# Output projection of an encoder block: eight half-size products become seven, with merged blocks summed in place and operands in reused rooms

## The chip, the cores and the metric

The kernel runs on one core of a Trainium2 chip. The core has a matrix engine (TensorE, PE in the profile, with its weight loads as PEld), an elementwise engine (VectorE, DVE), an engine for activations and copies (ScalarE, ACT), a programmable engine that is used for elementwise work here (GpSimd, POOL) and a queue that issues the DMAs (SyncE, SP). The on-chip memory is SBUF; products are accumulated in PSUM, which has eight banks of 128 x 512 float32 values. The metric is the time of one execution in microseconds on the device; the median of several runs is what counts.

## The reference

One encoder block on 1024 tokens of width 1024, with 16 meta tokens in front. Two attention branches give `y_a` and `y_b` (1024 x 512 each for the real tokens). What the change touches is the merge of the branches, the output projection, the residual, the norm and the beginning of the feed-forward:

```python
    merged = jax.nn.sigmoid(ga) * (y_a @ w_ba) + jax.nn.sigmoid(gb) * (y_b @ w_bb)
    return merged @ w_o
...
def swiglu(h, w_gate, w_up, w_down):
    return (jax.nn.silu(h @ w_gate) * (h @ w_up)) @ w_down
...
        h = h + mixer_block(rms_norm(h, norm_mix[layer]), w_in[layer],
...
        h = h + swiglu(rms_norm(h, norm_ffn[layer]), w_ff_gate[layer], w_ff_up[layer], w_ff_down[layer])
    return rms_norm(h, norm_final)[:, N_META:]
```

`w_o` is 1024 x 1024, the feed-forward is 2816 wide, all values are float32.

## The kernel before

Every product is made from float32 operands that are split into a high and a low half of type float32r: `split` writes the high half on ScalarE (L117) and the difference on VectorE or GpSimd (L118). A product of two operands is then three matmuls, high x high, high x low and low x high. The unit of work is a matmul of a 128 x 128 stationary block with a 128 x 512 moving block.

The program is traced in one function. Instructions of TensorE stay in the order of the program text from L1015 on (a manual order), and from L1370 on those of all engines do. Elsewhere a scheduler puts each engine's instructions in order, earlier text first among those that it takes to be ready. Each engine then works through its own list strictly in that order. Tiles come from pools: a tile with a tag takes one of the tag's rooms, and its first writer waits until the readers of the room's last tenant are done.

The stages around the change, in order:

1. *Branch b* (L1017): for each of eight blocks `o` of 128 output columns and two halves of the tokens, twelve matmuls (`branch_mm`, L780) into a PSUM bank; the result times the sigmoid of a gate goes to `tb_row(o, tk)` (L1021). The rows of `tb` lie in a tile of their own (`o` of 0 to 3) and in two rooms of `lowpool` (4 to 7).
2. *Branch a and merge* (L1037): the same for the other branch, in the order `order_a`: for blocks 0 to 3 and then 4 to 7, the first half of the tokens, then the second. VectorE multiplies with the gate (L1041), GpSimd adds the row of branch b (L1042), and the sum is split into `mT` (16 splits, the low half on VectorE). In the second half of this loop `prep_wo(0, c)` loads and splits the left half of `w_o`.
3. *Output projection* (L1241): `out_mm` multiplies one block of 128 tokens with one half (`q`) of the columns of `w_o`, over eight blocks `c` of the inner dimension, three matmuls each. Three rounds take four token blocks at a time, (q, group) = (0, 0), (0, 1), (1, 0); in the round (0, 1) `prep_wo(1, c)` prepares the other half of `w_o`. The last four token blocks follow one at a time (L1252). After a round `out_add` (L1075) adds the PSUM result to `h2`, which was loaded from `x`.
4. *Norm and turning*: `norm_f(t)` (L1199) squares and sums on ScalarE (L1202), takes the inverse root on GpSimd (L122, L123) and scales on VectorE (L1204) into a raw tile `xn`; `h2` goes out to DRAM. `turn_f(t)` (L1208) transposes eight 128 x 128 blocks on TensorE into two PSUM banks. For token blocks 0 to 3 it writes the operands `b11` and `b21` (L1222, L1223) and a copy `kept` (L1225). For blocks 4 to 7 it writes `b22` and four sums (L1233 to L1236). Blocks 0 to 4 are turned between the last output steps, blocks 5 to 7 between the first feed-forward products (`AFTER`, L1341), where `split_t` also splits the sums into the operands `t_ops`.
5. *Feed-forward, first half* (L1342): gate (`i` = 0) and up (`i` = 1) projections for eleven pairs `fp` of column blocks, each by seven half-size products in place of eight (`product_f`, twelve matmuls, L1293). The first, second and fifth product open a PSUM bank (`b1`, `b2`, `b3`); the others accumulate on in one of these. The products 1 and 2 of the first three pairs come first, so that the first-product banks of three pairs are open at a time. `result` empties banks: L1302 and L1307 add a kept copy, L1309 multiplies. `prepare` makes the weight operands up to eight ahead (`weights`, `load_unit`).
6. *Feed-forward, second half* (L1443): the down projection, also as seven products, and the final norm.

Rooms matter for the change. `op_tile` has eight rooms for split weights and `raw_tile` five for raw loads and for `xn`. `WB_BUFS` is the number of split branch weights held at a time (L773). `ps_bank` (L958) hands out any of eight PSUM banks. Separate pools hold `mT`, `gffn` and the first feed-forward weights (`mpool`), the operands `b11`, `b21`, `b22` (`bops`), eight tiles for `h2`, `kept` and the sums (`h2pool`), the operands of the sums (`topool`), the copies of products (`pcopy`, seven rooms) and the weight sums (`spool`).

## Time and profile before

| | us |
|---|---|
| median of three runs | 1451.38 |
| lowest and highest of the three | 1447.25, 1451.52 |
| profiled execution, whole | 1446.1 |
| profiled execution, first to last instruction (span) | 1444.3 |

The mean granted clock of TensorE in the profiled execution is 0.997. In a row of the page or of the windows, an engine's name is followed by its busy time and its number of instructions. In a group of instructions the row has line, engine, operation, written tile, read tiles, shapes and count, then the busy time and the mean of one in ns, then the engine's idle time just before and what ended it. In the order of instructions a row has its start, its time, the engine and line, and in brackets the idle time before it and what ended that. The chain of waits goes back from the last instruction to what released each one.

The stages in the trace: branch b from 622.0 us, branch a from 665.6, the first output matmul at 709.3 and the last at 800.6, the feed-forward from 801.6, the down projection from about 1227.

### The profile page before, as it was taken

The numbers are of one execution on the slowest core, as the hardware profiler recorded it, in microseconds if no ns is written. First come the engines' busy times: TensorE is split into PE (matmuls) and PEld (weight loads), VectorE is DVE, ScalarE is ACT, GpSimd is POOL, SyncE is SP. The second block draws the span as 40 slices with busy tenths as digits, with TensorE's granted clock in tenths as the row PEclk, the third lists the DMA queues.
The fourth block names the chain that finished last, engine by engine and source line by source line (L and its number), as shares of the span: only waits on it lengthen the run. The fifth ranks groups of instructions, "written<-read, shape, count | busy, mean of one in ns | idle before, by whom it ended". The sixth has DMA issues, their size and how long they took to land.

```text
span 1444.3 us, 21160 instructions
## 1 busy us (share of the span) xinstructions
PE 1422.8 (99%) x7279; PEld 1221.2 (85%) x7279; DVE 899.2 (62%) x1624; ACT 679.6 (47%) x1290; POOL 641.3 (44%) x605
## 2 busy tenths in 40 slices
PE   8999999999999999999999999999999999999997
PEld 6988989988898999888888878888888888888886
DVE  7478536637697989624614966554555553787567
ACT  6366535545665656544413643333333333444454
POOL 5599127743333333334522665544544452000444
PEclk9999999999999999999999999999999999999999
DMA  8467658986557473576612534333332332964443
GB/s 244 90 209 237 193 162 265 288 281 213 190 169 257 147 227 125 190 256 209 216 34 88 152 104 161 109 102 110 102 102 96 110 102 102 331 208 140 124 129 139
DMA packets 188891, 242.41 MB, mean 168 GB/s; under 512 B 18208, under 2 KB 115936, under 8 KB 188784
## 3 DMA queue, kind: packets, MB, share of 16 engines
q1 hardware_dynamic: 188784, 241.07, 52.6%
q8 instruction: 57, 0.93, 0.3%
q14 instruction: 50, 0.41, 0.1%
HBM read 157.45 MB, written 77.00 MB: 162 GB/s over the span
## 4 chain that ended last, share of the span: by engine, by line
PE 81%; POOL 6%; DVE 5%; issue 4%; DMA 2%; ACT 1%; POOLq 0%; SPq 0%; DVEq 0%; ACTq 0%
PE pg L1293 28%; PE pd L1387 9%; PE pg L737 7%; PE po L1070 6%; PE ppa L780 6%; PE aps L796 3%; PE pp_qb L214 3%; POOL oa L118 3%; PE apy L835 3%; PE pp_ka L214 2%; PE pp_va L214 2%; PE apt L822 2%; PE pp_qa L214 2%; PE bpt L356 1%; PE bpy L362 1%
## 5 line engine op out<-in xcount | busy, mean ns | idle before, releaser
L118 POOL TENSOR_TENSOR wop<-wf,wop 128x512 fp32r<-128x512 f32 x128 | 172.6, 1353 | 165.5 <-ACT wop L117 149.6
L1293 PE MATMUL pg<-t,wop 128*128 128x512 f32 x1056 | 242.6, 389 | 0.0
L1293 PEld LDWEIGHTS pg<-t,wop 128*128 128x128 f32 x1056 | 198.3, 188 | 41.1
L1387 PE MATMUL pd<-ob,oa 128*128 128x512 f32 x924 | 209.9, 389 | 0.4 <-POOL oa L118 0.4
L1387 PEld LDWEIGHTS pd<-ob,oa 128*128 128x128 f32 x924 | 173.4, 188 | 36.8 <-POOL oa L118 0.8
L1293 PE MATMUL pg<-b,wop 128*128 128x512 f32 x792 | 185.6, 392 | 2.3 <-DVE c L1302 2.3
L1293 PEld LDWEIGHTS pg<-b,wop 128*128 128x128 f32 x792 | 149.5, 189 | 34.1 <-issue 2.4
L737 PE MATMUL pg<-hT_hi,gop 128*128 128x512 f32 x384 | 142.7, 396 | 0.0
L118 POOL TENSOR_TENSOR oa<-ra,oa 128x512 fp32r<-128x512 f32 x33 | 44.0, 1335 | 170.1 <-ACT oa L117 168.6
L117 ACT ACTIVATE wop<-wf 128x512 fp32r<-128x512 f32 x128 | 80.2, 631 | 82.9 <-PE pg L1293 48.6
L118 POOL TENSOR_TENSOR gop<-gr,gop 128x512 fp32r<-128x512 f32 x48 | 63.3, 1319 | 116.4 <-ACT gop L117 102.6
L117 ACT ACTIVATE oa<-ra 128x512 fp32r<-128x512 f32 x77 | 48.7, 632 | 105.9 <-PE pd L1387 45.1
L804 ACT ACTIVATE as<-as,amn 128x1040 f32<-128x1040 f32 x64 | 74.5, 1164 | 46.9 <-DVE amn L799 42.8
L1128 DVE TENSOR_TENSOR s<-wf,wf 128x512 f32<-128x512 f32 x22 | 25.0, 1138 | 108.1 <-DMA wf<-in_w_ff_gate_dram 58.0
L796 PE MATMUL aps<-ak,aq 128*128 128x392 f32 (+1 forms) x384 | 90.0, 330 | 1.3 <-DVE amn L799 0.6
L1070 PE MATMUL po<-woh,mT 128*128 128x512 f32 x384 | 88.0, 390 | 0.0
L1070 PEld LDWEIGHTS po<-woh,mT 128*128 128x128 f32 x384 | 71.9, 188 | 14.8
L796 PEld LDWEIGHTS aps<-ak,aq 128*128 128x128 f32 x384 | 69.6, 189 | 15.0 <-DVE amn L799 2.2
L737 PEld LDWEIGHTS pg<-hT_hi,gop 128*128 128x128 f32 x384 | 72.7, 189 | 11.2 <-DVE gk L742 0.2
L343 POOL TENSOR_SCALAR bs<-bs,bdn 128x432 f32<-128x432 f32 (+1 forms) x64 | 41.4, 666 | 85.5 <-DVE bdn L341 73.4
L737 PE MATMUL pg<-hT_lo,gop 128*128 128x512 f32 x192 | 76.0, 396 | 0.0
L807 POOL TENSOR_SCALAR as<-as,adn,neglam 128x1040 f32<-128x1040 f32 x32 | 38.8, 1214 | 62.5 <-DVE adn L805 43.9
(287 smaller groups left out, 3099.0 us busy)
## 6 DMA issues: line engine op xcount, KB each, us to landing
ra<-aop SPq DMA_DIRECT2D x77, 256.0 KB, 2.6
wf<-in_w_ff_gate_dram SPq DMA_DIRECT2D x24, 512.0 KB, 4.0
wf<-in_w_ff_up_dram SPq DMA_DIRECT2D x24, 512.0 KB, 3.9
aop<-as SPq DMA_DIRECT2D x44, 256.0 KB, 2.1
w_c<-in_w_in_dram SPq DMA_DIRECT2D x17, 512.0 KB, 5.7
aop<-c SPq DMA_DIRECT2D x33, 256.0 KB, 2.0
ts_d<-to SPq DMA_DIRECT2D x16, 512.0 KB, 3.7
gw<-in_w_in_dram SPq DMA_DIRECT2D x32, 256.0 KB, 3.9
```

The costliest lines, as they stand in the source:

```text
L117: nc.scalar.activation(hi, src, AF.Copy)
L118: lo_eng.tensor_tensor(lo, src, f32(hi), ALU.subtract)
L214: nc.tensor.matmul(ps[:, :n], a[:, c, :], b[:, c, at:at + n], start=(c == 0 and i == 0), stop=(c == DC - 1 and i == 2))
L343: nc.gpsimd.tensor_scalar(st[:, r, :W], st[:, r, :W], dn[:, r:r + 1], 1.0, ALU.mult, ALU.mult)
L737: nc.tensor.matmul(ps, op[:, a, c], quad(b, *act)[:, c], start=(p in (2, 5, 1) and c == 0 and i == 0), stop=(p in (2, 3, 4) and c == 3 and ...
L780: nc.tensor.matmul(ps, w[:, a, j, :], src(j, b, tk), start=(j == 0 and n == 0), stop=(j == 3 and n == 2))
L796: nc.tensor.matmul(ps[:, :n], qs[m][:, t * P:(t + 1) * P], ks[m][:, vv, k0:k0 + n], start=(vv == 0), stop=(vv == 1))
L804: nc.scalar.activation(s[m][:, 0:L], s[m][:, 0:L], AF.Exp, bias=low, scale=-1.0, accum_out=dn[:, m:m + 1])
L835: nc.tensor.matmul(py[:, cols], v[:kp, a, k, :], at_[:kp, k, b, :], start=(k == 0 and j == 0), stop=(k == 8))
L1070: nc.tensor.matmul(ps, mT[:, c, a, t * P:(t + 1) * P], wos[q, c][:, b], start=(c == 0 and n == 0), stop=(c == DC - 1 and n == 2))
L1293: nc.tensor.matmul(ps, op[:, x, c, :], b[:, y, c, :], start=(p in (1, 2, 5) and c == 0 and n == 0), stop=(p in (4, 2, 3) and c == 3 and n ...
L1387: nc.tensor.matmul(ps[u], oa[:, a, u * P:(u + 1) * P], ob[:, b, :], start=(p in (1, 2, 5) and j == 0 and k == 0), stop=(p in (2, 3, 4) and ...
```

## The change

The output projection is cut into halves of the tokens, of the inner dimension and of the columns. Seven products of half-size operands, in the order `OUT` = 1, 5, 6, 3, 7, 2, 4, take the place of eight. Each product has four inner blocks, four token blocks and three matmuls. On the merged side, products 1, 3 and 2 use blocks of the merge as they are, and 5, 6, 7 and 4 use sums, which `m_sum` makes on VectorE in the place of the blocks. On the weight side, 5, 6, 3 and 7 use sums, made in `prep_wo`. Products 1, 6, 7 and 4 accumulate in one set of four banks (`xb`), 5 and 3 in another, 2 in a third; `out_add` reads a bank after each product. Products 2 and 4 go one token block at a time, and blocks 0 to 4 are turned among them, block 4 behind the last step.

The merge loop goes by quarters: second half of the tokens for blocks 0 to 3, first half for 0 to 3, first half for 4 to 7, second half for 4 to 7. GpSimd adds in the row of `tb`, and each quarter's split goes to the operand of one product (the second quarter by way of `m_sum(5, o)`). `load_ya` and `split_ya` take the second half of the tokens first.

The rooms: PSUM has two tags of four banks; the gate takes the one and the up projection the other, the turnings among the output steps use the first, and everything else alternates. `m_ops` and the operands of the feed-forward share rooms (`oa` to `oe`, the room of `tb`, and `gp`, which also holds `gffn`, the weight sums `s_f` and the first feed-forward weights). `h2` of blocks 4 to 7, the sums of the turned blocks and `s1` use the rooms of the split branch weights, four instead of five. The copies of products lie in two rooms of `lowpool`, four copies to a tile.

```diff
-WB_BUFS = 5
+WB_BUFS = 4
...
-    def ps_bank(name):
-        return bank(psum3, "bank", name, 8)
+    n_bank = [0]
+
+    def ps_bank(name, tag=None):
+        if tag is None:
+            tag = ("bankA", "bankB")[n_bank[0] % 2]
+            n_bank[0] += 1
+        return bank(psum3, tag, name, 4)
...
+    def prep_wo():
+        if n_wo[0] == len(order_o):
+            return
+        p, c = order_o[n_wo[0]]
+        n_wo[0] += 1
+        tt = nc.vector.tensor_tensor
+        raw = raw_tile(f"wo_{p}_{c}")
+        if p in (1, 6):
+            src = wo_block(raw, 0, c, 0)
+        elif p in (3, 2):
+            src = wo_block(raw, 0, 4 + c, 0)
+        elif p == 5:
+            a, b = wo_block(raw, 0, c, 1), wo_block(raw, 1, 4 + c, 1)
+            src = s_f[c]
+            tt(src, a, b, ALU.add)
+        elif p == 7:
+            src, b = wo_block(raw, 0, c, 0), wo_block(raw, 1, c, 1)
+            tt(src, src, b, ALU.subtract)
+        else:
+            src = wo_block(raw, 0, 4 + c, 1)
+        if p == 6:
+            tt(s_f[c], s_f[c], src, ALU.subtract)
+            src = s_f[c]
+        elif p == 3:
+            tt(src, src, s_f[c], ALU.subtract)
+        wos[p, c] = op_tile(f"woh_{p}_{c}")
+        split(wos[p, c][:, 0], wos[p, c][:, 1], src, nc.gpsimd)
...
+    def m_split(p, c, src):
+        split(m_ops[p][:, 0, c], m_ops[p][:, 1, c], src, nc.vector)
+
+    def m_sum(p, c):
+        tt = nc.vector.tensor_tensor
+        t, bx, b21 = tb_row(c, Y), tb_row(c, X), tb_row(4 + c, X)
+        if p == 5:
+            tt(t, t, bx, ALU.subtract)
+        elif p == 6:
+            tt(t, tb_row(4 + c, Y), t, ALU.subtract)
+        elif p == 7:
+            tt(bx, t, bx, ALU.subtract)
+            t = bx
+        else:
+            tt(b21, b21, t, ALU.subtract)
+            t = b21
+        m_split(p, c, t)
...
-    order_a = [(o, h) for b in range(0, DC, 4) for h in range(2) for o in range(b, b + 4)]
+    order_a = [(o, half) for b, halves in ((0, (1, 0)), (4, (0, 1))) for half in halves for o in range(b, b + 4)]
...
-        nc.gpsimd.tensor_tensor(gt, gt, tb_row(o, tk), ALU.add)
-        split(mT[:, o, 0, tk], mT[:, o, 1, tk], gt, nc.vector)
+        nc.gpsimd.tensor_tensor(tb_row(o, tk), tb_row(o, tk), gt, ALU.add)
+        if n // 4 == 1:
+            m_sum(5, o)
+        else:
+            m_split((1, None, 3, 2)[n // 4], o % 4, tb_row(o, tk))
         if n >= 8:
-            prep_wo(0, n - 8)
+            prep_wo()
...
+    xb = [ps_bank(f"po_x{u}", "bankB") for u in range(4)]
+    yb_ = [ps_bank(f"po_y{u}", "bankA") for u in range(4)]
+    for p in (1, 5, 6, 3, 7):
+        pss = yb_ if p in (5, 3) else xb
+        for c in range(4):
+            for u in range(4):
+                out_mm(pss[u], p, u, c)
+            prep_wo()
+            if p == 1:
+                m_sum(6, c)
+        for u in range(4):
+            if p == 1:
+                out_add(xb[u], 4 + u, 0)
...
+            else:
+                out_add(xb[u], u, 1)
+                norm_f(u)
+        if p == 1:
+            m_ops[7] = half_op(opool, "oa", "mo7")
+            for c in range(4):
+                m_sum(7, c)
+        elif p == 5:
+            m_ops[4] = half_op(opool, "ob", "mo4")
+            for c in range(4):
+                m_sum(4, c)
...
+    def second(p, u):
+        ps = ps_bank(f"po_z{u}", "bankA") if p == 2 else xb[u]
+        for c in range(4):
+            out_mm(ps, p, u, c)
+        out_add(ps, 4 + u, 0 if p == 2 else 1)
+        if p == 4:
+            norm_f(4 + u)
+
+    for p, u, k in ((2, 0, None), (2, 1, None), (2, 2, 0), (2, 3, None), (4, 0, 1), (4, 1, 2), (4, 2, 3), (4, 3, 4)):
+        second(p, u)
+        if k is not None:
+            turn_f(k, ("bankA", "bankA"))
     prepare(2 * 2)
...
+    def p_tile(name):
+        i = n_copy[0] % 4
+        if i == 0:
+            m = n_copy[0] // 4 % 2
+            copies[0] = lowpool.tile([P, 4, 512], F32, tag=f"k{m}", name=f"copies_{name}", bufs=1)
+        n_copy[0] += 1
+        return copies[0][:, i]
...
-            u[which] = ps_bank(f"pg_{nm}_{p}")
+            u[which] = ps_bank(f"pg_{nm}_{p}", ("bankA", "bankB")[i])
```

More of the change, by code (lines that the diff above doesn't have):

```diff
@@ L1028, in encoder_block @@
     for j in range(4):
-        split_ya(1, j, yapool)
-    mpool, close_mpool = pool("mpool", "right")
-    mT = mpool.tile([P, DC, 2, S], F32R, name="mT")
-    gffn = row(mpool, norm_ffn, D, "gffn")
-    first_f = [mpool.tile([P, 1024], F32, name=f"first_f{i}") for i in range(2)]
+        split_ya(0, j, yapool)
+    gpool2, close_gp = pool("gp", "right")
+    gp = gpool2.tile([P, 4096], F32, tag="gp", name="gp", bufs=1)
+    gffn = gp[:, 0:1024]
+    nc.sync.dma_start(gffn, norm_ffn.broadcast_to([P, D]))
@@ new lines, in encoder_block, with half_op @@
+    s_f = [gp[:, 1024 + 512 * i:1536 + 512 * i] for i in range(4)]
+    first_f = [gp[:, 3072:4096], gp[:, 1024:2048]]
+    opool, close_ops = pool("ops", "right")
+    def half_op(p, tag, name):
+        return p.tile([P, 2, 4, 512], F32R, tag=tag, name=name, bufs=1)
+    OUT = (1, 5, 6, 3, 7, 2, 4)
+    m_ops = {1: half_op(opool, "oa", "mo1"), 5: half_op(opool, "ob", "mo5"), 3: half_op(opool, "oc", "mo3"), 6: half_op(opool, "od", "mo6")}
+    order_o = [(p, c) for p in OUT for c in range(4)]
@@ new lines, in encoder_block, with wo_block @@
+    wos, n_wo = {}, [0]
+    def wo_block(raw, at, row, col):
+        part = raw[:, at * 512:at * 512 + 512]
+        nc.sync.dma_start(part, w_o[row * P:row * P + P, col * 512:col * 512 + 512])
+        return part
+    def prep_wo():
[25 more added lines that the diff above has]
+        split(wos[p, c][:, 0], wos[p, c][:, 1], src, nc.gpsimd)
@@ L1214, in turn_f @@
         for b in range(2):
-            pt = four(ps_bank(f"ptn_f{t}_{b}"))
+            pt = four(ps_bank(f"ptn_f{t}_{b}", tags[b]))
             for c in range(4):
@@ L1228, in turn_f @@
             return
-        kept, more = held.pop(u), h2_tile(f"ts_{u}")
+        kept, more = held.pop(u), wide_tile(f"ts_{u}")
         left, low = four(kept[:, 0:512]), four(kept[:, 512:])
@@ L1357, in encoder_block @@
     close_cpool()
[L1358 to L1361 removed]
+    close_ypool()
+    close_low()
+    close_e()
+    close_ops()
+    close_gp()
     ypool, close_y = pool("ypool2")
```

97 lines of the change are left out of this document (36 added, 61 removed).

## The prediction

> **What bounds the kernel now.** I read the page first, then the stretches around the output projection (busy time by windows), then the order of instructions where the feed-forward begins. Here is the page's span and its first row of busy time, and the chain of waits from the branch products on:
>
> ```profile
> span 1444.3 us, 21160 instructions
> PE 1422.8 (99%) x7279; PEld 1221.2 (85%) x7279; DVE 899.2 (62%) x1624; ACT 679.6 (47%) x1290; POOL 641.3 (44%) x605
> ...
> 622.43 87.08 PE ppa L780 x384
> 709.50 70.73 PE po L1070 x312
> ```
>
> TensorE is the bound: nothing but its own products stands in the chain for 158 us. So matmuls taken away come off the time, as long as nothing else becomes late. The other engines, stretch by stretch (columns: window, its length, then PE, PEld, DVE, ACT and POOL busy with counts, granted clock, DMA share, GB/s):
>
> ```profile
> 665.50:709.00 43.50, 43.50 (x194) 36.02 (x193) 28.66 (x34) 23.30 (x40) 28.80 (x20) 1.00 0.65 197
> 709.00:755.00 46.00, 46.00 (x205) 38.09 (x204) 11.56 (x16) 8.63 (x14) 14.65 (x12) 1.00 0.33 116
> 755.00:780.00 25.00, 25.00 (x112) 20.70 (x111) 5.61 (x7) 4.27 (x8) 4.63 (x8) 1.00 0.21 84
> 801.60:833.50 31.90, 29.67 (x139) 24.05 (x137) 29.93 (x36) 19.61 (x36) 22.58 (x16) 1.00 0.62 173
> 815.00:835.00 20.00, 17.71 (x75) 13.96 (x74) 20.00 (x25) 12.79 (x23) 15.05 (x9) 0.96 0.42 132
> 833.50:837.00 3.50, 3.44 (x8) 2.82 (x9) 3.50 (x6) 1.10 (x2) 0.44 (x1) 0.51 0.02 5
> ```
>
> The output projection (709 to 801) is the emptiest stage: VectorE has 17.2 of 71 us of work up to 780. The beginning of the feed-forward is the opposite: VectorE is full from 815 to 835, and there TensorE does wait. From the order of instructions:
>
> ```profile
> 817.65 13.92 PE L1293 MATMUL pg<-b,wop 128*128 128x512 f32 x60 [0.30 <-DVE c L1302]
> 833.56 4.82 PE L1293 MATMUL pg<-b,wop 128*128 128x512 f32 x13 [1.99 <-DVE c L1302]
> ...
> 832.73 0.68 DVE L1302 TENSOR_TENSOR c<-pg,p 128x512 f32<-128x512 f32 x1
> ```
>
> The eleventh product of the feed-forward waits until VectorE has emptied a PSUM bank at L1302, behind the splits and sums of the transposed activations. The window 833.5 to 837 shows what such a stop costs besides: the granted clock is 0.51 for 3.5 us, another 1.7 us.
>
> **Removed: 48 matmuls.** Eight products of 48 become seven, 384 to 336. The price is the spacing in an undisturbed stretch:
>
> ```profile
> L780 PE MATMUL ppa<-ya,wbha x192: 389/389/396, 665.8 to 709.1; 128*128 128x512 f32 x192
> L1070 PE MATMUL po<-woh,mT x384: 387/389/476, 709.3 to 800.6; 128*128 128x512 f32 x192
> ```
>
> 43.3 us over 191 steps is 0.227 us each; 48 of them are **-10.9 us**. One product is 10.9 us, one 12-matmul step 2.72 us. This term is certain; its bounds are what VectorE gives back.
>
> **Added: sums and splits under the output products.** The merged side gets 16 two-input sums (5, 6, 7, 4) and 12 more split pairs (28 for 16); the weight side 16 sums and 12 more split pairs; there are 28 additions into h for 16, and 20 more weight loads. Prices, from the groups by line of 709 to 802 and the DMA issues of 640 to 840:
>
> ```profile
> L118 POOL TENSOR_TENSOR woh<-wo,woh 128x512 fp32r<-128x512 f32 x8 | 10.3, 1293 | 27.5 <-ACT woh L117 27.5
> L1075 DVE TENSOR_TENSOR h<-h,po 128x512 f32<-128x512 f32 x15 | 10.2, 686 | 50.1 <-PE po L1070 50.1
> L1042 POOL TENSOR_TENSOR gt<-gt,yb_raw 128x512 f32<-128x512 f32 x4 | 5.5, 1376 | 5.2 <-DVE gt L1041 5.2
> L117 ACT ACTIVATE woh<-wo 128x512 fp32r<-128x512 f32 x8 | 5.1, 632 | 30.7 <-PE po L1070 30.7
> L118 DVE TENSOR_TENSOR mT<-gt,mT 128x512 fp32r<-128x512 f32 x5 | 4.9, 972 | 4.3 <-ACT mT L117 4.3
> L1041 DVE TENSOR_TENSOR gt<-gt,ppa 128x512 f32<-128x512 f32 x3 | 2.0, 675 | 0.0
> ...
> wo<-in_w_out_dram SPq DMA_DIRECT2D x16, 256.0 KB, 3.2
> h<-in_x_dram SPq DMA_DIRECT2D x8, 512.0 KB, 6.2
> ```
>
> ScalarE's 24 more activations (24 x 0.63 = 15 us) fit into its 58 idle us of 709 to 780. The 20 loads (5.2 MB at 3.2 us to landing) lie where the DMA share is 0.21 to 0.33, a product ahead of use. The eight loads of x now wait for rooms of the branch weights and of ya0, up to the merge's end, and the SyncE queue holds the weight loads of products 6 and 3 behind them; the first result needs x 10.9 us later and its bank is wanted again only 21.8 us later. Cost of both: nothing; if that slack were gone, about one landing, 6 us.
>
> VectorE is the question. A two-input operation between SBUF tiles takes 0.68 us alone, but stretches where GpSimd runs (order of instructions; the last row is of the chain of waits):
>
> ```profile
> 816.40 9.84 POOL L118 TENSOR_TENSOR wop<-wf,wop 128x512 fp32r<-128x512 f32 x6
> 820.41 0.67 DVE L1234 TENSOR_TENSOR ts<-ptn_f,ts 128x512 f32<-128x512 f32 x1
> 823.32 1.78 DVE L1236 TENSOR_TENSOR kept<-kept,ts 128x512 f32<-128x512 f32 x1
> 829.12 0.68 DVE L1235 TENSOR_TENSOR kept<-ts,kept 128x512 f32<-128x512 f32 x1
> ...
> 828.00 1.20 DVE t L118 x2
> ```
>
> Operations that read PSUM (L1234) stay at 0.67 under the same GpSimd work; back to back they follow at 0.60. The ledger runs to the start of product 7, four products (43.5 us) into the stage: VectorE must have done 12 weight sums (6, 3, 7), 12 merged sums (6, 7, 4) with 12 lower halves, 36 x 0.60 = 21.6; 12 additions into h, 7.2; the tail of the merge, 4.9 + 2.0 as now: 35.7 us. GpSimd has 12 splits (12 x 1.29 = 15.5) and 5.5 of the merge's tail, 21 us. What part of it blocks VectorE? In the full stretch 815 to 835, 25 operations at 0.60 are 15.0 of 20.0 busy us, so 5.0 of GpSimd's 15.05, a third. 35.7 + 7 = 42.7 against 43.5: it just fits. For the earlier check (product 6 needs its sums and bank 21.8 us in, with the merge's backlog and early-started sums ahead of the additions into h) I take **+1 us**. Bounds: nothing, to all 21 us blocking, 56.7 - 43.5 = 13.2. Queued behind a blocked VectorE are the additions into h, and TensorE waits for them, since products 6, 3 and 7 accumulate on in the same banks.
>
> **Moved: the turning of token block 4, and the banks.** Now block 4 is turned ahead of the last output step, and its sums run under that step:
>
> ```profile
> 795.52 0.68 DVE L1233 TENSOR_TENSOR ts<-ptn_f,kept 128x512 f32<-128x512 f32 x1
> 797.04 1.28 DVE L1204 SCALAR_TENSOR_TENSOR xn_f<-h,rstd_f,gffn 128x1024 f32<-128x1024 f32 x1
> 798.23 0.69 DVE L1223 TENSOR_TENSOR b<-ptn_f,b 128x512 fp32r<-128x512 f32 x1
> 798.83 0.68 DVE L1234 TENSOR_TENSOR ts<-ptn_f,ts 128x512 f32<-128x512 f32 x1
> 799.55 1.73 DVE L1235 TENSOR_TENSOR kept<-ts,kept 128x512 f32<-128x512 f32 x1
> 800.85 1.04 PE L1218 MATMUL ptn_f<-ident,xn_f 128*128 128x128 f32 x8
> 801.21 1.77 DVE L1236 TENSOR_TENSOR kept<-kept,ts 128x512 f32<-128x512 f32 x1
> 801.64 5.73 PE L1293 MATMUL pg<-b,wop 128*128 128x512 f32 x24
> ```
>
> Afterwards block 4 is turned behind the last step (a step there is 2.72 instead of 5.44 us), so what VectorE did by 801.64 joins the queue that is full anyway: of the four sums (4.9 us) all but the 1.3 us that already lie behind 801.64, so 3.6, and one norm (1.28) with one split (0.69), 2.0. Before, L1302 ends 31.8 us behind the feed-forward's first product, and the eleventh product starts 31.9 behind it. After, counted from the end of the last output step: 31.8 + 3.6 + 2.0 - 2.0 (VectorE's idle time in 801.6 to 833.5, filled) = 35.4. The banks make it worse by a step: gate products have four of their own, three of them held by the first products of pairs 0, 1 and 2, so the tenth product, not the eleventh, needs the bank that L1302 empties. It starts at about 35.6, the eleventh at 38.3; two turnings (2 x 1.04) precede the first product, so that is 36.2 behind it instead of 31.9: **+4.3 us**. The half-rate window follows the stop in both. Bounds: 0 (the bank is emptied in time) to 6.3 (the idle time does not fill).
>
> [...]
>
> **Costed at nothing:** four branch-weight tiles for five (the tile of o = 4 comes free three products, 8.2 us, ahead of use, against a split of 0.63 + 1.3 us); copies in groups of four (a group is wanted again at the earliest some five products after its last reader, 13 us); the gate, first-unit and operand rooms (their last readers are a product back); two sets of four banks later on, where gate and up alternate as now; rooms of the down projection (30 us ahead). If one cover is gone, that is a product's wait, 2.7 us.
>
> **Sum:** -10.9 + 1.0 + 4.3 = -5.6. The profiled execution took 1446.1 (span 1444.3 and 1.8 around it), which would become 1440.5. It was 5.3 us below the median of the three runs, 1451.38; I apply the change to the median: **1445.8 us**.
>
> **Rivals.**
> (B) VectorE is never late: -10.9, 1440.5. For it: 17.2 of 71 us in use now. Against: the full stretch at 815.
> (C) Slower: GpSimd's splits block VectorE's sums outright in the output stage, products 6, 3 and 7 each wait for their banks, 13.2 us in all, plus 1.7 for one half-rate window: -10.9 + 4.3 + 14.9 = +8.3, 1459.7. It decides once the waits pass 6.6 us, a blocked share of 0.69 instead of 0.33. For it: operations of 1.7 to 1.8 us, and in 665 to 709 both engines are already two thirds busy, with eight sums more to come there. Against: the share measured in a full stretch.
> (D) Given back: the same waits at a third of that size, 5 us with their half-rate window, -10.9 + 4.3 + 5 = -1.6, 1449.8.
>
> **Chances.** Forecast 0.42 (its own range 1442 to 1449), B 0.15, C 0.18, D 0.25. A measurement here tells apart about 0.3%, 4.4 us. Faster by more: four fifths of the forecast, all of B, a little of D: 0.52. Within: the rest of the forecast, most of D, a little of C: 0.29. Slower: the rest, 0.19. The range leaves out a tenth at each side: 1439 (all of B with the runs' scatter) to 1457 (most of C).
>
> **What would show it.** 336 output matmuls, 7231 in all. Right: output products at 0.227 us without a gap over 1 us before products 6, 3 and 7, and a wait for L1302's successor at the tenth feed-forward product with about 36 us from the first product to the eleventh. VectorE about 98% busy over the first four output products. Wrong: gaps ahead of products 6, 3, 7 released by the additions into h or by GpSimd's splits (C, D); no wait at the beginning of the feed-forward (B); a steady feed-forward that is no longer gapless from the fifteenth product on, which none of these cases has.

## The result and the profile after

The changed kernel took 1470.09 us (median of four runs, 1467.71 to 1472.15) against 1451.21 us before (four runs, 1447.25 to 1451.52): a ratio of 1.0136 with an interval of 1.011 to 1.0162. It is 18.9 us slower where 5.6 us less had been forecast, and it lies above the range. From the page of the changed kernel, the span, the first row of busy time, and two groups (operation, count | busy us, mean ns | idle time just ahead and what ended it):

```profile
span 1465.9 us, 21204 instructions
PE 1419.9 (97%) x7231; PEld 1215.3 (83%) x7231; DVE 949.2 (65%) x1680; ACT 696.4 (48%) x1314; POOL 660.2 (45%) x617
...
L1386 PE MATMUL pg<-b,wop 128*128 128x512 f32 x792 | 188.0, 396 | 9.7 <-ACT wop L115 5.8
...
L1130 PE MATMUL po_x<-woh,mo 128*128 128x512 f32 x192 | 47.9, 405 | 13.1 <-DVE gt L1105 13.1
```

7231 matmuls, 48 fewer: the change does what it says. But PE is now idle 13.1 us ahead of the first output products, ended each time by L1105, the multiplication of the *merge*, and 9.7 us in the feed-forward (2.3 before). Cut by the first matmul of each stage, the time stands like this:

| us | up to the b branch | b branch, merge | output stage | feed-forward | down, to the last matmul |
|---|---|---|---|---|---|
| before | 622.3 | 87.1 | 92.3 | 425.3 | 210.3 |
| after | 623.4 | 89.5 | 98.6 | 437.1 | 210.3 |
| difference | +1.1 | +2.5 | +6.3 | +11.8 | 0 |

The first column is the scatter of runs: no instruction differs there, and it moves between 622.3 and 627.4 in the runs below. The output stage should have *lost* 10.9 us. It gained 6.3, so some 17 us were lost in it.

The same kinds of stretches as before the change (window, length, then PE, PEld, DVE, ACT and POOL busy, granted clock, DMA share, GB/s); the first is the merge, the second and third are the beginning of the output stage, the fourth is the beginning of the feed-forward, and the last lies around the waits of the first output product:

```profile
669.00:712.70 43.70, 41.53 (x183) 34.02 (x182) 37.95 (x44) 20.89 (x36) 27.92 (x19) 1.00 0.67 212
712.70:758.70 46.00, 32.90 (x134) 25.95 (x133) 40.77 (x49) 17.65 (x30) 24.29 (x16) 0.85 0.48 159
758.70:783.70 25.00, 25.00 (x112) 20.71 (x111) 7.62 (x12) 7.07 (x12) 11.79 (x10) 1.00 0.24 74
811.31:843.20 31.89, 27.96 (x128) 23.07 (x127) 31.89 (x39) 19.95 (x36) 18.44 (x13) 0.95 0.60 174
718.60:732.20 13.60, 4.75 (x11) 3.01 (x10) 13.60 (x16) 5.19 (x9) 7.97 (x6) 0.51 0.69 251
```

VectorE went from 11.56 to 40.77 us of the first 46 us, and the granted clock is 0.51 for 13.6 us in there. What VectorE does instead of emptying banks is seen in its order of instructions around the start of the stage at 712.7:

```profile
701.22 0.68 DVE L1068 TENSOR_TENSOR gp<-gp,wo 128x512 f32<-128x512 f32 x1
701.82 0.67 DVE L1105 TENSOR_TENSOR gt<-gt,ppa 128x512 f32<-128x512 f32 x1
702.41 1.47 DVE L1068 TENSOR_TENSOR gp<-gp,wo 128x512 f32<-128x512 f32 x1
...
705.51 0.68 DVE L1084 TENSOR_TENSOR tb<-tb 128x512 f32<-128x512 f32 x1
706.11 0.68 DVE L1068 TENSOR_TENSOR gp<-gp,wo 128x512 f32<-128x512 f32 x1
706.71 0.67 DVE L1105 TENSOR_TENSOR gt<-gt,ppa 128x512 f32<-128x512 f32 x1
...
717.31 0.67 DVE L1105 TENSOR_TENSOR gt<-gt,ppa 128x512 f32<-128x512 f32 x1
...
718.04 1.02 PE L1130 MATMUL po_x<-woh,mo 128*128 128x512 f32 x3 [4.26 <-DVE gt L1105]
...
723.79 1.65 PE L1130 MATMUL po_x<-woh,mo 128*128 128x512 f32 x3 [4.74 <-DVE gt L1105]
...
728.83 0.67 DVE L1105 TENSOR_TENSOR gt<-gt,ppa 128x512 f32<-128x512 f32 x1
...
729.55 5.71 PE L1130 MATMUL po_x<-woh,mo 128*128 128x512 f32 x18 [4.11 <-DVE gt L1105]
```

Between two multiplications that free a bank stand sums for products 6 (L1068) and 5 (L1084), work that the source has later or that nobody waits for yet: the planner that places instructions on the engines took them ahead. The last multiplication starts 15.9 us into the stage (before: 5.5 us). Product 1 takes the second set of banks, which holds the merge's products 9, 11, 13 and 15, so it waits three times for the *last* ones. In the feed-forward two products wait:

```profile
827.60 0.68 DVE L1293 TENSOR_TENSOR ts<-ptn_f,kept 128x512 f32<-128x512 f32 x1
...
828.42 15.28 PE L1386 MATMUL pg<-b,wop 128*128 128x512 f32 x60 [3.93 <-DVE ts L1293]
...
848.68 0.68 DVE L1395 TENSOR_TENSOR c<-pg,copies_p 128x512 f32<-128x512 f32 x1
...
849.51 6.85 PE L1386 MATMUL pg<-b,wop 128*128 128x512 f32 x17 [5.80 <-ACT wop L115]
```

The fifth product wants the bank of a turned block, the tenth the one that L1395 empties (the profile names ACT's split; but PE's first weight load starts 0.12 us behind the end of L1395 at 849.36, as it starts 0.11 us behind the end of L1293 at the fifth product, and with one set of banks the wait is gone).

### The profile page after: what moved, and what is told of

It is laid out like the page before. It is cut to its first block, busy times and chain, and to the rows that moved or that the text cites. A ratio compares the mean times of both kernels' runs of the same rounds, so it can differ in the third digit from the quotient of the medians.

```text
span 1465.9 us, 21204 instructions
## 1 busy us (share of the span) xinstructions
PE 1419.9 (97%) x7231; PEld 1215.3 (83%) x7231; DVE 949.2 (65%) x1680; ACT 696.4 (48%) x1314; POOL 660.2 (45%) x617
## 4 chain that ended last, share of the span: by engine, by line
PE 77%; DVE 8%; POOL 6%; issue 5%; DMA 2%; ACT 2%; SPq 0%; POOLq 0%; DVEq 0%; ACTq 0%
PE pg L1386 28%; PE pd L1479 9%; PE pg L735 8%; PE aps L794 3%; PE pp_qb L212 3%; PE apy L833 3%; POOL oa L116 3%; PE po_x L1130 3%; PE ppa L778 3%; PE pp_ka L212 2%; PE pp_va L212 2%; PE apt L820 2%; PE pp_qa L212 2%; PE po_y L1130 1%; PE bpt L354 1%
## 5 line engine op out<-in xcount | busy, mean ns | idle before, releaser
L794 PE MATMUL aps<-ak,aq 128*128 128x392 f32 (+1 forms) x384 | 89.5, 328 | 2.5 <-DVE amn L797 2.4
L1188 DVE TENSOR_TENSOR s<-wf,wf 128x512 f32<-128x512 f32 x22 | 20.8, 947 | 106.4 <-DMA wf<-in_w_ff_up_dram 55.5
L331 DVE CUSTOM_DVE_ANT_0 bs<-bps,tbx,nsink 128x432 f32<-128x432 f32 (+1 forms) x64 | 38.2, 622 | 37.3 <-PE bps L329 28.4
L1130 PE MATMUL po_x<-woh,mo 128*128 128x512 f32 x192 | 47.9, 405 | 13.1 <-DVE gt L1105 13.1
```

Source lines behind the costliest of these rows:

```text
L794: nc.tensor.matmul(ps[:, :n], qs[m][:, t * P:(t + 1) * P], ks[m][:, vv, k0:k0 + n], start=(vv == 0), stop=(vv == 1))
L1130: nc.tensor.matmul(ps, m_ops[p][:, a, c, u * P:(u + 1) * P], wos[p, c][:, b], start=(p in (1, 5, 2) and c == 0 and n == 0), stop=(p in (3, ...
```

## The experiments

Three causes act on the same waits: the two sets of banks (T), the order that sums take ahead of work that PE waits for (H), and the amount of work on VectorE, with GpSimd's operations blocking it (P; later split by what an operation of GpSimd takes from VectorE, as estimated in e8's expectation: 0.68 us, the weak lock L; 1.18 us, the strong lock S; nothing, the amount alone, A). `issue_after` in the diffs keeps what stands in its block behind the named instruction. All times in one table; the ratio is to the kernel before as measured beside each run, with its interval; then three stages as above. e11 leaves out a part of the computation, so it is a probe and not a version.

| run | us | ratio | branches | output | feed-forward |
|---|---|---|---|---|---|
| after | 1470.1 | 1.0136 (1.011 to 1.0162) | 89.5 | 98.6 | 437.1 |
| e1 one set | 1457.6 | 1.0058 (1.004 to 1.0076) | 90.8 | 92.2 | 428.9 |
| e2 merge on other set | 1463.9 | 1.0099 (1.0084 to 1.0114) | 91.3 | 92.1 | 437.0 |
| e3 sums behind merge | 1460.1 | 1.0071 (1.0054 to 1.0087) | 87.1 | 92.1 | 437.1 |
| e4 = e1 + e3 | 1452.8 | 1.0029 (1.0018 to 1.0039) | 87.1 | 92.5 | 428.9 |
| e5 = e4 + additions first | 1453.4 | 1.0032 (1.002 to 1.0043) | 87.1 | 91.1 | 428.6 |
| e7 = e4 + early turning | 1452.7 | 1.0026 (1.0016 to 1.0035) | 87.1 | 91.6 | 429.2 |
| e6 = e5 + early turning | 1453.1 | 1.0022 (1.0012 to 1.0031) | 87.1 | 90.3 | 429.0 |
| e8 = e6 + splits on VectorE | 1446.2 | 0.9979 (0.9969 to 0.999) | 87.1 | 85.0 | 429.2 |
| e11 = e6, halves left out | 1443.6 | 0.9958 (0.9943 to 0.9973) | 87.1 | 81.5 | 428.7 |
| e12 = e6 + sums in b branch | 1459.5 | 1.0069 (1.0054 to 1.0085) | 102.7 | 81.5 | 429.2 |
| e13 = e12 + all splits on VectorE | 1456.9 | 1.006 (1.0042 to 1.0078) | 103.0 | 81.5 | 427.4 |
| e14 = e8 + first units on VectorE | 1446.3 | 0.9983 (0.9973 to 0.9993) | 87.1 | 85.1 | 428.5 |
| e15 = e1 + splits on VectorE | 1452.0 | 1.0018 (1.0007 to 1.0029) | 89.1 | 88.1 | 428.6 |
| e16 = after + splits on VectorE | 1469.1 | 1.0139 (1.0124 to 1.0155) | 89.5 | 99.6 | 436.0 |
| e17 = before + splits on VectorE | 1450.0 | 1.0005 (0.9994 to 1.0016) | 87.1 | 92.3 | 425.3 |

**e1, one set of eight banks.**

```diff
-            tag = ("bankA", "bankB")[n_bank[0] % 2]
-            n_bank[0] += 1
-        return bank(psum3, tag, name, 4)
+        return bank(psum3, "bank", name, 8)
```

> One PSUM tag of eight banks, as before the change; all else as changed. Theory T (the two sets of four banks are the cause: the first output product needs the banks of merge products 9, 11, 13 and 15, the last of which VectorE empties 16 us into the stage): the first four banks now come from merge products 8 to 11, so the 13.9 us of gaps in the first output product shrink to one wait of 2 to 3 us, the fifth feed-forward product no longer waits (4.2 us) and the tenth or eleventh waits about 2 us less: 1450 to 1452, level with the kernel before. Theory H (VectorE's order, weight sums and merged sums ahead of the merge's multiplications): the same place improves, but VectorE's multiplication of the last merge product still runs 16 us behind TensorE. Theory P (VectorE with GpSimd's blocking has no room for the sums at all): the gaps move from product 1 to products 5 and 6, 1465 or more.

**e2, two sets, but the merge's products 8 to 11 take the set that product 1 will want.**

```diff
-            tag = ("bankA", "bankB")[n_bank[0] % 2]
+            tag = ("bankB", "bankA")[n_bank[0] // 4 % 2] if n_bank[0] < 32 else ("bankA", "bankB")[n_bank[0] % 2]
```

> The two sets of four banks stay, but the merge products 8 to 11 use the set that the first output product takes, and 12 to 15 the other. Touches the output stage alone. Theory T: gaps in the first output product from 13.9 to about 3 us and the half-rate window with them, about -13 us: 1457; the feed-forward's beginning unchanged (waits of about 4 and 6 us ahead of its fifth and tenth product). Theory P: the gaps come back ahead of products 5 and 6, under 4 us gained, 1467 or more.

e2 has e1's output stage and the changed kernel's feed-forward. So the sets cost at two places: at the start of the output stage by *which* banks come next (98.6 to some 92 in either run), and in the feed-forward by there being two sets (437.0 against 428.9: 8.1 us; in the changed kernel the tenth product waits 5.80 us there, with a granted clock of 0.52 from 848.20 to 855.20 us). Both runs fall short of theory T's forecast, because product 6 now waits 4.52 us in both, so the work in front of it is still there, and because e1's fifth feed-forward product still waits 3.93 us.

**e3, the sums behind the merge's multiplications, and e4, both.**

```diff
+        mults.append(nc.vector.tensor_tensor(gt, gt, ps, ALU.mult).ins)
...
         if n >= 8:
-            prep_wo()
+            with tc.issue_after(mults[n]):
+                prep_wo()
...
-            prep_wo()
-            if p == 1:
-                m_sum(6, c)
+            with tc.issue_after(mults[15]):
+                prep_wo()
+                if p == 1:
+                    m_sum(6, c)
```

(the sums of products 7 and 4 likewise, behind multiplication 15)

> Banks as changed; the weight sums of product 5 are queued on VectorE behind the merge's multiplication of the same step, and all sums of products 6, 7, 3 and 4 behind the last multiplication. Theory H: VectorE's last merge multiplication comes 5 to 7 us behind TensorE instead of 16, the gaps in the first output product shrink from 13.9 to about 5 us (the bank of merge product 15 is still wanted in the first round), the 2.6 us wait for a branch weight in the merge goes: 1456 to 1459. Theory T alone: no more than 3 us gained. Theory P: the gaps come back ahead of products 6 and 3, where the sums are then late: 1467 or more.

> One set of eight banks and the sums queued behind the multiplications. T and H together: no gap over 1 us in the output stage or in the merge, the feed-forward's beginning with one wait as in the kernel before plus what block 4's turning adds (about 36 us from its first to its eleventh product): 1443 to 1447, faster than the kernel before. Theory P: gaps of several us ahead of products 6, 3 or 7, 1452 or more.

The merge's wait is gone in both (89.5 to 87.1, as before the change): it was the order, and four branch-weight tiles instead of five cost nothing. The output stage comes to some 92 in both, as in e1 and e2, so e4 misses T and H's forecast and lands where P put it. In e4 product 1 runs without a gap, and all of the wait stands ahead of product 6, as its order of instructions shows:

```profile
730.46 1.78 DVE L1083 TENSOR_TENSOR tb<-tb 128x512 f32<-128x512 f32 x1
732.16 1.78 DVE L1086 TENSOR_TENSOR yb_raw<-yb_raw,tb 128x512 f32<-128x512 f32 x1
...
742.16 1.27 DVE L1131 TENSOR_TENSOR h<-h,po_x 128x512 f32<-128x512 f32 x2
742.98 2.47 PE L1126 MATMUL po_x<-woh,mo 128*128 128x512 f32 x5 [8.01 <-DVE h L1131]
```

The additions into h, which free product 1's banks, stand behind sums for products 7 and 4. Order again, or too much work?

**e5, the additions first; e6 and e7, block 4 turned earlier, with and without that.**

```diff
-            with tc.issue_after(mults[15]):
+            with tc.issue_after(mults[{1: 15, 5: 19}.get(p, 23)]):
                 prep_wo()
...
-    for p, u, k in ((2, 0, None), (2, 1, None), (2, 2, 0), (2, 3, None), (4, 0, 1), (4, 1, 2), (4, 2, 3), (4, 3, 4)):
+    for p, u, k in ((2, 0, ()), (2, 1, ()), (2, 2, ()), (4, 0, (0,)), (4, 1, (1,)), (2, 3, (2,)), (4, 2, (3, 4)), (4, 3, ())):
```

(mults 16 to 23 are the additions of products 1 and 5; the sums of 7 wait for 19, those of 4 for 23. The first hunk is e5, the second e7, both are e6.)

> The changed kernel with one set of eight banks and the sums behind the merge's last multiplication (as in the run before), and besides with the additions into h ahead of the next sums: product 7's merged sums and product 3's weight sums may be issued only behind the last addition of product 1, those of products 4 and 7 behind the last of product 5. Order (H): the 8.4 us gap ahead of product 6 falls to about 1 us and none over 1 us comes ahead of products 3 and 7; the output stage is 83 to 85 us instead of 92.5, and the time is 1443 to 1446 us, ratio 0.997. Capacity (P): the work doesn't fit whatever its order; the gap only moves, to ahead of products 3 or 7 as waits for operands (splits at L117/L118 or sums), the stage stays at 91 to 93 us and the time at 1451 to 1454. Either way the fifth feed-forward product still waits its 4.2 us.

> As the run above, and block 4 turned earlier: blocks 0, 1 and 2 between the steps of the second half of the output stage (behind the second, third and fourth step of eight), 3 and 4 behind the seventh, as many steps ahead of the feed-forward as the kernel before has. If the fifth feed-forward product waits because block 4's sums run behind the last step, the 4.2 us gap and the half-rate clock behind it vanish: feed-forward and down projection 635 to 637 us instead of 639, 3 to 5 us less than the run above, so 1438 to 1442 with order (H) and 1447 to 1450 with capacity (P). If the queue of VectorE is full there whatever comes first, the gap moves into the last output steps or stays, and nothing is won.

> Only the earlier turning, with the additions into h still behind the sums. The 8.4 us gap ahead of product 6 stays; the fifth feed-forward product's 4.2 us vanishes if the late turning is its cause: 1448 to 1450 us, 3 to 5 less than one bank set with the sums behind the merge (ratio 0.999). If the turning isn't the cause, 1452 to 1454 (ratio 1.003).

Order (H) fails here. The 8.01 us ahead of product 6 become 3.15 there and 3.21 ahead of product 7, the stage gains 1.4 us of some 10, and the time stays. (The expectations count a wait from the start of one matmul to the start of the next, 0.39 us more than the brackets of the rows, and call the second wait product 3's; by the order of the matmuls it is product 7's.) The early turning doesn't pay either, and by e7's own forecast its 1452.7 us mean that the late turning isn't the cause. The fifth feed-forward product's 3.93 us vanish in e7, but they vanish in e5 as well, where block 4 is turned as late as in e4. A wait appears further on each time: 3.42 us ahead of the eleventh product in e5, and 0.94, 2.92 and 1.03 us ahead of the tenth, eleventh and twelfth in e6. VectorE is full at both places: in e6 the windows show it (from the first output product to product 7, and the feed-forward's beginning), and in e5 VectorE and GpSimd work in turns:

```profile
712.00:764.00 52.00, 46.62 (x193) 37.73 (x192) 51.45 (x56) 22.10 (x37) 36.40 (x21) 0.93 0.56 187
...
802.00:837.00 35.00, 30.85 (x145) 24.83 (x144) 35.00 (x42) 21.00 (x38) 21.67 (x15) 1.00 0.56 158
```

```profile
720.66 1.74 POOL L116 TENSOR_TENSOR woh<-gp,woh 128x512 fp32r<-128x512 f32 x1
721.17 1.78 DVE L1063 TENSOR_TENSOR gp<-gp,wo 128x512 f32<-128x512 f32 x1
722.36 1.74 POOL L1101 TENSOR_TENSOR yb_raw<-yb_raw,gt 128x512 f32<-128x512 f32 x1
722.87 1.78 DVE L1081 TENSOR_TENSOR tb<-yb_raw,tb 128x512 f32<-128x512 f32 x1
```

In these rows of e5 each of VectorE's two operations between SBUF tiles ends 0.55 us behind GpSimd's and takes 1.78 us instead of 0.68. In e6's window VectorE is busy 51.45 of 52 us with only 56 operations, 0.92 us each. If each of GpSimd's 21 operations there held VectorE up for its whole length, that would be up to 21 x 1.29 = 27 us, an estimate from the prediction's row for one.

**e8, the output weights' halves on VectorE; e11, twelve of GpSimd's halves left out.**

```diff
-        split(wos[p, c][:, 0], wos[p, c][:, 1], src, nc.gpsimd)
+        split(wos[p, c][:, 0], wos[p, c][:, 1], src, nc.vector)
```

> The version with one bank set, additions first and block 4 turned early, and besides the lower halves of the output weights made on VectorE instead of GpSimd (28 operations). In its profile VectorE has no idle time from the first output product to product 7: 61 operations in 52.3 us while GpSimd does 23. Read as a whole, GpSimd's operations take (52.3 - 61 x 0.60) / 23 = 0.68 us each from VectorE (L, weak lock): then moving 18 of them at 0.60 changes next to nothing, 1451 to 1454 us. Read from the pairs (1.78 us for an operation of VectorE behind one of GpSimd, against 0.60), each costs 1.18 (S, strong lock): moving 18 saves up to 9 us of VectorE's queue, the gaps ahead of products 6 and 3 (3.8 and 2.7 us) fall below 1 and the time to 1445 to 1448. If GpSimd doesn't block VectorE at all (A, amount alone), VectorE's queue grows by 11 us and the time to 1460 or more.

> The same version, with part of the computation left out: the lower halves of the weights of products 6, 3 and 7 are not differences but a second rounded copy made by ScalarE, so GpSimd has 12 operations fewer between the merge and product 7, and VectorE's own work is unchanged. Blocking (L or S): 12 x 0.68 to 12 x 1.18, 8 to 14 us less in VectorE's queue, both gaps ahead of products 6 and 3 (6.5 us with 1.7 us of half clock) vanish or fall below 1.5 us, 1444 to 1447 us. Amount alone (A): the gaps stay, 1452 to 1454 us.

The same window in e8, then in e11:

```profile
712.00:764.00 52.00, 49.92 (x215) 39.73 (x214) 50.33 (x79) 21.00 (x36) 5.03 (x3) 1.00 0.55 182
```

```profile
712.00:764.00 52.00, 52.00 (x231) 43.07 (x230) 46.61 (x66) 29.41 (x53) 19.81 (x13) 1.00 0.64 213
```

VectorE does 79 operations in less time than 56, at 50.33 / 79 = 0.64 us each. So the 56 of e6 are 35.7 us of its own work, and the other 15.8 us are what 21 operations of GpSimd took from it, 0.75 each: between the weak lock (0.68) and the strong one (1.18), and more than the 0.64 that a half costs where it is made on VectorE itself. (The 61 and 23 operations of the expectation count those at its windows' bounds twice. The stretch holds 56 and 21, and its own sum then gives 0.89 instead of 0.68.) Taken up to the start of product 7, VectorE does 56 operations in 51.3 us in e6, and 69 in 44.3 us in e8. Moving work onto the *fuller* engine gained 5.3 us in this stage. Of the 3.5 us that e8 keeps above a stage without waits, about half lie at product 7, which waits 1.45 us for a half that VectorE now makes. In e11, with 8 operations fewer on GpSimd in this window, the stage has no wait left at all: 81.5 us. That is 10.8 less than before, the whole of the forecast's first term. A (amount alone) is refuted by both.

**e12, the sums of weights made in the b branch, and e13, with all those splits on VectorE.**

```diff
+        tt(w22, w12, w22, ALU.add)
+        tt(w12, w11, w12, ALU.subtract)
+        tt(w11, w22, w11, ALU.subtract)
+        tt(w21, w21, w11, ALU.subtract)
+        for p, part in ((5, w22), (7, w12), (6, w11), (3, w21)):
+            nc.sync.dma_start(ws_d[p, c], part)
...
+        if o % 2:
+            sums_wo(o // 2)
```

> The same version, with the 16 sums of output weights (products 5, 6, 3, 7) made during the b branch, where VectorE is busy 12.9 of 44 us and GpSimd 11.6, stored to DRAM and loaded again as single tiles. VectorE has 12 sums fewer from the first output product to product 7 (49 for 61): at 0.60 each 7.2 us, with their share of blocking up to 9. If the queue of VectorE is the bound there, the gaps ahead of products 6 and 3 fall from 6.5 to 0 to 2 us and the half clock behind them goes: 1444 to 1448 us, a ratio of 0.997 to 0.9995. 8 MB more of transfers in the b branch (DMA share 0.5 to 1.0 there) may cost waits for gates and branch weights, 0 to 4 us. If the bound were the bank supply or the transfers, the gaps would stay: 1453 or more.

> The run above, and besides all splits of output weights, of the transposed sums and of the feed-forward's first units on VectorE instead of GpSimd. Strong lock (S): the waits at the tenth and eleventh feed-forward product (4.6 us) shrink to 1 to 2 and none is left in the output stage, 1440 to 1445 us. Weak lock (L): within 2 us of the run above. Amount alone (A): 5 to 10 us longer than the run above.

Windows of e12, both branches and then the output stage, and the wait that dominates the first:

```profile
624.74:727.47 102.73, 91.95 (x385) 72.39 (x384) 57.54 (x74) 44.16 (x74) 44.72 (x31) 0.98 0.81 267
727.47:808.95 81.48, 81.48 (x384) 67.97 (x383) 62.30 (x75) 39.67 (x73) 50.76 (x42) 1.00 0.41 145
```

```profile
652.04 0.63 ACT L115 ACTIVATE wbhb<-wbrb 128x512 fp32r<-128x512 f32 x1 [0.17 <-DMA wbrb<-in_w_branch_b_dram]
...
652.72 0.73 PE L778 MATMUL ppa<-yb,wbhb 128*128 128x512 f32 x2 [1.36 <-ACT wbhb L115]
```

With 12 sums fewer the output stage is gapless, which with e8 (85.0 us for e6's 90.3) says that VectorE's queue is the bound there. The price was far above the 0 to 4 us expected, 15.7 us: branch weights land late (ScalarE waits 10.5 us in all for those of branch b) where transfers and stores were added (DMA share 0.81 over both branches). Which of the two holds them up was not tried. As a version it is a miss. e13 is 2.7 us shorter than e12, a little more than the weak lock's forecast of within 2 us and far from the strong lock's total.

**e14 to e17: what is left, and what the blocking alone explains.** e14 also makes the halves of the transposed sums and of the first feed-forward units on VectorE (`nc.vector if fp == 0 else nc.gpsimd`); e15, e16 and e17 put e8's one-word edit into e1, the changed kernel and the kernel before.

> The version with the output weights' lower halves on VectorE, and besides those of the transposed sums and of the feed-forward's first units, which GpSimd makes in the stretch where products 10 and 11 of the feed-forward still wait (1.3 and 3.3 us, with 1.7 us of half clock). Strong lock (S): the pairs of 1.78 and 1.74 us there go, the two waits fall from 4.6 to 1 to 2.5 us and the time from 1446 to 1442 to 1445 us. If VectorE is full there whoever makes the halves: 1445 to 1448.

> The changed kernel with one set of eight banks and the output weights' halves on VectorE, its order otherwise as the change has it (sums ahead of the merge's multiplications, block 4 turned late). One set alone gave 1457.6 us. If the lock (S) is what made the hoisted order costly, 8 us less: 1449 to 1452. If the order costs by itself, its gap of 4.9 us ahead of product 6 and the merge's 2.5 us stay: 1454 to 1458.

> The changed kernel with only the output weights' lower halves on VectorE. If the lock of GpSimd's splits alone carries the loss in the output stage, its three waits in product 1 go: 1459 to 1462 us (the feed-forward's 11.8 us and some of the merge's wait stay). If the order and the two bank sets carry it, the waits stay and it is 1466 to 1470.

> The kernel before with its 16 output weight splits on VectorE, nothing else changed: a control for the runs that beat it. Its VectorE is busy 17 of 71 us in the output stage, so there is nothing to relieve but 8 splits under the merge: 1447 to 1451 us, ratio 0.998 to 1.001. If it falls below 1446, the gain of those runs is not the change's.

e16: without the other two edits the relief is worth nothing; product 1 still waits for the merge's last banks, and the output stage is even 1 us longer. e15: with one set it is worth 4.2 us of the stage (92.2 to 88.1), and the hoisted order (sums taken ahead) still costs the merge 2.0 us. The stage is 3.1 us longer than e8's, of which 0.8 to 0.9 go with the later turning, as e5 against e6 and e4 against e7 show. e17: the kernel before gains nothing, so e8's 3 us are the change's. e14: the feed-forward's wait mostly moves (0.7 us less than e8; between e12 and e13 1.9). In the windows around its last two waits GpSimd has no operation at all, and VectorE is full:

```profile
827.00:829.60 2.60, 0.69 (x4) 0.22 (x2) 2.60 (x5) 1.70 (x3) 0.00 (x0) 1.00 0.00 0
829.60:836.50 6.90, 4.78 (x20) 3.68 (x21) 6.90 (x13) 5.39 (x10) 0.00 (x0) 1.00 0.00 0
```

e8 is the version that beats both kernels, with e14 level: 1446.2 us, 0.2% below before and 1.6% below the changed kernel.

## Why the prediction was wrong

**-10.9 for 48 matmuls: right.** Where nothing waits (e11, e12, e13) the output stage is 81.5 us, 10.8 less than before.

**+1.0 for waits of the output stage: wrong by 16.** It had three faults.
First, the ledger, the count of what VectorE must do before product 7. Its own work was right (35.7 us forecast; 35.7 from e6's count at e8's price). What failed is "a third" of GpSimd's time, and the count of GpSimd's operations (some 16; 21 ran). The stretch that the third came from held 9 operations of GpSimd that took 5.0 us from VectorE, 0.56 each; here each took 0.75, in all 15.8 us instead of 7. This is rival C's mechanism, and in microseconds it passes C's mark: 15.8 is above the 0.69 x 21 = 14.5 from which C lost the gain. As a share of GpSimd's own time it is 15.8 of 21 x 1.29, or 0.58, which stays below C's 0.69, so the mark is passed only because more operations ran. C had a chance of 0.18. With the bank sets and the order mended, e6 shows the size: two waits of 3.41 and 2.29 us, a granted clock of 0.88 in the 24.2 us behind the first, and a stage 8.8 us above gapless.
Second, the ledger took VectorE's order from the source ("the tail of the merge, 4.9 + 2.0 as now"). The sums were taken ahead of the multiplications, the last of these started 15.9 us into the stage instead of 5.5, and the merge itself lost 2.5 us (e3).
Third, the banks of the first product weren't costed. The "two sets of four banks later on" stood under "Costed at nothing" as a matter of gate and up alternating; which four of the eight product 1 gets was not asked. With the late tail it got the latest (e1, e2: some 6.4 us). The second and third fault share those 6.4 us: mending either one ends at about 92.2, mending both at 92.5, because the ledger's 10 us come behind them. So no single share for each can be given.

**+4.3 for the feed-forward's start: mechanism half right, size 11.8.** With one set of banks the stage is 3.3 to 3.9 us longer than before in e1, e4, e5, e6, e7 and e8. That is near the 4.3, but partly by luck: e6, e7 and e8 turn block 4 as early as before, and the stage stays as long. VectorE's order of instructions says what is in the way there. From the start of the first feed-forward product to that of the eleventh it does 35 operations before and 40 in e6 and e8. Two of the five more are block 4's last sums (L1291 and L1292 in e6), which started ahead of the first product before; these the term had. The other three are weight sums of later units (L1185, L1186), which stood behind L1302 before, and which the prediction left out. Here are the two last of them ahead of the bank that the eleventh product wants in e6, and then the order before:

```profile
834.44 0.68 DVE L1186 TENSOR_TENSOR wf<-s,wf 128x512 f32<-128x512 f32 x1
835.04 0.68 DVE L1185 TENSOR_TENSOR wf<-wf 128x512 f32<-128x512 f32 x1
835.65 0.68 DVE L1399 TENSOR_TENSOR copies_p<-pg,copies_p 128x512 f32<-128x512 f32 x1
```

```profile
832.73 0.68 DVE L1302 TENSOR_TENSOR c<-pg,p 128x512 f32<-128x512 f32 x1
...
835.02 1.27 DVE L1129 TENSOR_TENSOR wf<-wf 128x512 f32<-128x512 f32 x2
```

This is read from the order; no run moved these sums back, so the share of each stays open. The two sets cost 8.1 us on top, where the text gave them one step of 2.7: they did make the tenth product wait for L1302's successor, as said, but for 5.8 us, and the granted clock was 0.52 in the 7.0 us from 848.20 us. The fifth product's wait, for a turned block's bank, was not foreseen.

**Costed at nothing:** branch-weight tiles (e3 and e4: merge as before), loads of x and weights, copies and rooms: no wait of PE over 1 us in the changed kernel's output stage and feed-forward is put down to them. Only the banks were wrong among these.

**The clock:** the changed kernel's waits of 4 to 6 us cost more than themselves. The granted clock is 0.51 over the 13.6 us of product 1's three waits (4.26, 4.74 and 4.11 us), 0.55 in the 3.6 us from 827.70 us, around the end of the fifth feed-forward product's 3.93 us, and 0.52 in the 7.0 us from 848.20, around the end of the tenth's 5.80. The prediction's window from 833.5 us had shown 0.51 behind a wait of 1.99; its 1 us for the output stage holds nothing for that.

**Sum by measured terms:** +1.1 scatter, +2.5 order in the merge, -10.8 + 17.1 in the output stage, +11.8 in the feed-forward: 21.6 us of span (1465.9 - 1444.3).

## What to carry to other kernels

Before work goes to an engine "with room", price its neighbours: here each of GpSimd's operations cost VectorE more time (0.75 us, from e6 against e8) than VectorE needed to make such a half itself (0.64 in e8). Work that nobody waits for yet must be kept behind work that frees banks by an explicit order, since the planner doesn't follow the source; and when banks are divided into sets, ask of each first user which earlier reader its banks still wait for. A stage that sheds matmuls also sheds the cover under which other engines worked.

## What the runs showed of the hardware

In these runs the length of a wait doesn't by itself tell whether the clock is halved. The same product waits for the same release in e6 and in e8, 2.92 and 2.94 us, and the window behind it runs at 1.00 in the one and at 0.56 in the other (order of instructions and window of e6, then of e8):

```profile
836.38 3.06 PE L1385 MATMUL pg<-b,wop 128*128 128x512 f32 x12 [2.92 <-DVE copies_p L1399]
```

```profile
836.20:839.70 3.50, 3.06 (x12) 2.17 (x12) 3.50 (x5) 0.11 (x1) 2.37 (x2) 1.00 0.01 2
```

```profile
831.48 4.84 PE L1385 MATMUL pg<-b,wop 128*128 128x512 f32 x13 [2.94 <-DVE copies_p L1399]
```

```profile
831.60:835.20 3.60, 3.60 (x10) 2.81 (x11) 3.60 (x4) 0.32 (x1) 2.04 (x2) 0.56 0.00 0
```

In the changed kernel it is 1.00 behind the merge's wait of 2.17 us, 0.52 in 7.0 us around the end of the tenth product's 5.80, and 0.55 in 3.6 us around the end of the fifth's 3.93:

```profile
699.60:703.20 3.60, 3.54 (x16) 2.94 (x17) 3.60 (x4) 1.15 (x2) 2.31 (x2) 1.00 0.59 172
848.20:855.20 7.00, 5.69 (x14) 4.47 (x15) 3.19 (x5) 2.85 (x6) 5.65 (x4) 0.52 0.10 37
827.70:831.30 3.60, 2.88 (x7) 2.33 (x8) 3.60 (x5) 2.96 (x4) 3.60 (x3) 0.55 0.50 145
```

The record of the granted clock in the changed kernel's trace has half-rate stretches from 339.93 us (3.41 us long), 718.81 (13.65, the three waits of product 1, one after the other), 828.04 (3.41) and 848.52 (6.83); the kernel before has two, from 338.65 and 833.58 (3.41 each). Their lengths are 1, 2 and 4 times 3.413 us, and within each trace they start a multiple of 3.413 us apart. Only the last stretch of each trace, which reaches past the end of the span, has another length (5.03 and 5.18 us). Cut at these steps, the time around the two waits looks like this (e6, then e8; the first busy time is PE's):

```profile
831.69:835.10 3.41, 1.76 (x8) 1.12 (x6) 3.41 (x7) 1.23 (x2) 0.44 (x1) 1.00 0.00 0
835.10:838.52 3.42, 2.14 (x9) 1.77 (x10) 3.42 (x5) 1.10 (x2) 3.42 (x2) 1.00 0.01 2
```

```profile
828.60:832.01 3.41, 0.53 (x2) 0.49 (x3) 3.41 (x6) 2.18 (x4) 2.26 (x2) 1.00 0.00 0
832.01:835.42 3.41, 3.41 (x9) 2.65 (x8) 3.41 (x5) 0.54 (x2) 1.63 (x1) 0.50 0.00 0
```

e6's wait is shared between two steps, and TensorE is busy for 1.76 and 2.14 us of them. e8's lies in one step, which has 0.53 us of work, and the next step runs at half rate. The same cut over the traces of the kernel before and of the changed kernel, from 20 to 1420 us, gives 808 steps at full rate. In the 6 that were followed by a half-rate step TensorE was busy for at most 0.43 of the step, in all others for at least 0.53. So in these traces a wait's place in the steps decides, as far as it decides how busy one step is. In four of the 6 TensorE had worked for 0.23 to 0.43 of the step.
